# Seven-product blocks in a fixed interleaving, with two of their sums per step made by accumulating transfers

## The chip, the core and the metric

The kernel is one program on one core of a Trainium2 chip. The metric is the device time of one execution, in microseconds, as the median over several executions. The engines are named as in the profile: PE multiplies matrices (PEld is its weight load), DVE and ACT work element by element, POOL here issues the accumulating transfers and a few small operations, and SP issues the plain loads.

## The reference

Two layers of a decoder trunk on 256 tokens of width 2048, all in float32. Cut to what matters here:

```python
for l in range(2):
    h = rms_norm(x, norm1_g[l])
    z = h @ w_in[l]                      # the 1024 query columns of it are one of the blocks below
    ...                                  # gated spatial unit, windowed attention, out projection
    h2 = rms_norm(x, norm2_g[l])
    x = x + (silu(h2 @ w_gate[l]) * (h2 @ w_up[l])) @ w_down[l]     # w_gate, w_up: 2048 x 5632
```

## The kernel before

**The arithmetic.** A weight tile is 128 rows by 1024 values in float32 (two row groups j of 512 columns). `split2` (L117) makes two tiles of it: `wh`, rounded by a cast on ACT (L123), and `wl`, what the rounding left, by a subtraction on DVE (L124). Each product is then three matmuls of 512 columns (`mm3`, L158 to L161): high activations with `wh`, high activations with `wl`, low activations with `wh`. A *half unit* is one weight tile against one token tile: 6 matmuls. A *standard unit* (`unit`, L163) is one weight tile against both token tiles: 12 matmuls.

**Seven products in place of eight.** For the queries of a layer, and for ten of the eleven column blocks of the gate and up projections (`S_BLOCKS`), `seven` (L333) multiplies a 2 x 2 arrangement of activations (token tile by parity of the row group) with a 2 x 2 arrangement of weights (parity r by column block c, `src(r, c, i)`) with seven products in place of eight. There are four steps i, each with one tile of every weight block: b11 = src(0,0), b12 = src(0,1), b22 = src(1,1), b21 = src(1,0). The products need sums of weights: b11+b12, t2 = b11+b12+b22, b12+b22 and t2+b21. The sums of activations (`ext`) were made earlier. The products go into five PSUM banks (m0 to m4), and sums of the banks make the results (`out`, which for the gate and up projections is `gated`, L1057: silu of the one times the other).

**Where the sums are made.** In each step b11+b12 (L365) and t2 (L366) are additions on DVE. b12+b22 is an addition on DVE (L372) or, for the steps named in `by_dma`, a transfer from HBM issued on POOL that adds what it brings to what lies in SBUF (L368). `by_dma` is all four steps for the first layer's queries, steps 0 and 2 for the gate and up blocks, and no step for the second layer's queries. t2+b21 is always such a transfer (L374).

**What sets the order.** Generators yield unit by unit. The stretch of the gate, up and down projections draws half units from `s_stream` (L1069) and fills standard units of `w_down` and of the one remaining block in between, about 3 standard units for 10 half units (L1197). The queries of the first layer run between the standard units of keys, values and gating, at a set pace (`q_to`, L489). `later` puts small work at a set distance. After that a planner of the framework puts the instructions of each engine into a fixed order by its own model of their durations. Each engine and each queue then works through its instructions in that order, and waits at the first one whose inputs are missing.

**Buffers.** 8 tiles `raw` hold weights as loaded, 5 `wh` and 4 `wl` hold the split halves, 4 tiles (`spt`) hold t2. A load on SP waits until the last reader of the tile that was in its buffer is done. PSUM has 5 banks of the kind the seven products use.

Of the kernel before, what the change touches and what calls it, by code (L numbers as in the profile page):

```python
# [12 lines left out]
F32 = mybir.dt.float32  # L13
# [3 lines left out]
ALU = mybir.AluOpType  # L17
# [3 lines left out]
P = 128  # L21
# [13 lines left out]
NB = 512  # L35
# [6 lines left out]
S_BLOCKS = (1, 2, 3, 4, 5, 6, 7, 8, 9, 10)  # L42
# [28 lines left out]
EXT_AT = (6.5, 8, 11, 13, 16, 18, 21.5, 24)  # L71
MASK_AFTER = ((5, 5), (4, 4))
GATE_LOAD = ((24, 29), (5, 15))
PARTS = (
    "a0 a0 a1 a1 s a0 a0 s a1 s a1 s s s b0 s b0 s b0 s b0 s b1 s b1 s b1 s b1 s b2 b2 b2 b2 b3 b3 b3 b3",
    "a0 a0 a1 a1 a0 a0 s a1 a1 s b0 b0 s b0 s b0 s s b1 s b1 s b1 s b1 s s b2 s b2 s b2 b2 s b3 b3 b3 b3",
# [14 lines left out]
def trunk(ctx, tc, x, xt, w_in, w_q, w_out, w_oa, w_uh, w_gate, w_up, w_down, sgu_w, sgu_g, consts,  # L91
          band, out):
    nc = tc.nc
# [14 lines left out]
    def raw_load(src, parts=1):  # L108
        raw = wp.tile([P, 2, NB], F32, tag="raw", name="raw", bufs=8)
        n = 2 // parts  # L110
        for i in range(parts):
            nc.sync.dma_start(raw[:, i * n : (i + 1) * n, :], src[:, i * n : (i + 1) * n, :])
        return raw

    last_wl = [None]

    def split2(raw):  # L117
        wh = wp.tile([P, 2, NB], F32R, tag="wh", name="wh", bufs=5)
        wl = wp.tile([P, 2, NB], F32R, tag="wl", name="wl", bufs=4)
        step = 2 if clock[0] > 1 else 1  # L120
        for j in range(0, 2, step):
            src = raw[:, j : j + step, :]
            nc.scalar.copy(wh[:, j : j + step, :], src)  # L123
            last_wl[0] = nc.vector.tensor_tensor(  # L124
                wl[:, j : j + step, :], src, f(wh[:, j : j + step, :]), ALU.subtract
            )
        return wh, wl
# [5 lines left out]
    def later(delay, fn):  # L133
        pending.append((clock[0] + delay, next(serial), fn))

    def tick(w=1.0):
        clock[0] += w
        due = sorted((e for e in pending if e[0] <= clock[0]), key=lambda e: e[:2])
        pending[:] = [e for e in pending if e[0] > clock[0]]
        for e in due:  # L140
            e[2]()
# [16 lines left out]
    def mm3(acc, ah, al, wh, wl, first, last, again=False):  # L158
        nc.tensor.matmul(acc, ah, wh, start=first, stop=False, skip_group_check=again)  # L159
        nc.tensor.matmul(acc, ah, wl, start=False, stop=False, skip_group_check=again)  # L160
        nc.tensor.matmul(acc, al, wh, start=False, stop=last, skip_group_check=again)  # L161
# [50 lines left out]
    anchor = [None]  # L212
# [120 lines left out]
    def seven(src, pairs, ext, out, end=lambda sg: None, soon=False, by_dma=(), put_off=False):  # L333
# [78 lines left out]
        end([m0, c21])  # L412
        yield

    def seven_low(src, pairs, ext, done, tag="hT"):
        def half(raw, acc, op, i, first=False, stop=False):
            wh, wl = split2(raw)
# [62 lines left out]

    def q_product(lay, pairs, ext):
        q = {"k": 0}
        q["steps"] = seven(
            lambda r, c, i: w_q[lay, c, i, r], pairs, ext, lambda *a: q["out"](*a),
            soon=True, by_dma=range(4 if lay == 0 else 0),
        )
        return q

    def q_to(q, share):  # L489
# [32 lines left out]
    for lay in range(L):  # L522
# [526 lines left out]
        def act_later(b, sg, held=held, release=release):  # L1049
            for c in range(2):  # L1050
                def ready(c=c):
                    held.append((b, c, sg))
                    release()

                later(2 + c, ready)
# [3 lines left out]
            nc.vector.scalar_tensor_tensor(sg, c, nrstd2[t], sg, ALU.mult, ALU.mult)  # L1059

        def s_block(b, lay=lay, pairs2=pairs2, ext2=ext2, gated=gated, act_later=act_later):
            return seven(
                lambda r, c, i: (w_gate, w_up)[c][lay, b, i, r], pairs2, ext2, gated,
                lambda sg: act_later(b, sg), soon=b == S_BLOCKS[0], by_dma=(0, 2), put_off=True,
            )

        seven_done = [False]

        def s_stream(s_block=s_block):  # L1069
            for b in S_BLOCKS:  # L1070
                yield from s_block(b)

        seeds = []
        left = [NFF]
# [230 lines left out]
```

## Time and profile before

| | |
|---|---|
| median of the executions | 1907.07 us (1906.84 to 1908.11, 3 executions) |
| the profiled execution | 1906.77 us, its span 1905.1 us |
| PE busy | 1892.9 us, 99% of the span, 8624 matmuls and transposes |
| DVE busy | 1745.5 us, 92% |
| ACT busy | 1374.7 us, 72% |
| POOL busy | 183.9 us, 10% |
| moved by DMA | 463.12 MB, 243 GB/s |

The span is from the first to the last instruction of the profiled execution. A matmul's busy time is modelled and overlaps the next one's, so the distance of the starts tells more than the busy time. The gate, up and down stretches lie at about 330 to 925 us (first layer) and 1275 to 1870 us (second layer), the first layer's queries at about 30 to 120 us.

### The profile page before, as it was taken

How to read it: one execution, taken by the hardware profiler on the slowest of the kernel's cores; microseconds unless marked ns; L12 is line 12 of the kernel's file. 1: busy time of each engine (PE TensorE's matmuls, PEld its weight loads, DVE VectorE, ACT ScalarE, POOL GpSimd, SP SyncE). 2: the span in 40 equal slices, each digit the busy share in tenths (PEclk: the TensorE clock that was granted, in tenths of full speed). 3: DMA queues.
4: the chain of work that ended last, by engine and by line, in shares of the span. 5: the costliest groups of instructions: out<-in, count | busy, mean ns of one | idle time of the engine just before them, and what ended most of it. 6: DMA issues, size and time to landing. Idle time of an engine off the chain costs nothing.

```text
span 1905.1 us, 25218 instructions
## 1 busy us (share of the span) xinstructions
PE 1892.9 (99%) x8624; PEld 1544.2 (81%) x8624; DVE 1745.5 (92%) x1894; ACT 1374.7 (72%) x1860; POOL 183.9 (10%) x184
## 2 busy tenths in 40 slices
PE   9999999999999999999999999999999999999999
PEld 6887788888888888888888778888888888888887
DVE  7988989999999999999798888999999999999993
ACT  8668777677767776777776886766877677676774
POOL 0231001000100001000002200000000100010000
PEclk9999999999999999999999999999999999999999
DMA  9973668888977897889578648697789788888783
GB/s 356 261 284 133 194 202 243 248 247 276 271 238 245 270 290 228 243 261 290 185 217 291 191 153 237 212 280 224 233 282 288 227 254 264 270 249 251 249 277 110
DMA packets 129153, 463.12 MB, mean 243 GB/s; under 512 B 14336, under 2 KB 14720, under 8 KB 129024
## 3 DMA queue, kind: packets, MB, share of 16 engines
q1 hardware_dynamic: 105840, 378.54, 53.9%
q0 software_dynamic: 22464, 81.80, 23.7%
q8 instruction: 67, 1.10, 0.2%
q10 hardware_dynamic: 720, 1.18, 0.2%
q14 instruction: 62, 0.51, 0.1%
HBM read 459.36 MB, written 2.10 MB: 242 GB/s over the span
## 4 chain that ended last, share of the span: by engine, by line
PE 94%; ACT 2%; DVE 2%; issue 1%; DMA 0%; POOL 0%; SPq 0%; DVEq 0%; ACTq 0%; POOLq 0%
PE m L160 15%; PE m L159 15%; PE m L161 15%; PE dacc L160 11%; PE dacc L159 11%; PE dacc L161 11%; PE acc L160 4%; PE acc L161 3%; PE acc L159 3%; PE l L159 1%; PE l L160 1%; PE l L161 1%; PE ps_f L242 1%; PE ps_n L242 1%; DVE wl L124 1%
## 5 line engine op out<-in xcount | busy, mean ns | idle before, releaser
L123 ACT CAST wh<-raw 128x1024 fp32r<-128x1024 f32 (+1 forms) x794 | 814.0, 1050 | 366.5 <-DVE raw L365 165.7
L124 DVE TENSOR_TENSOR wl<-raw,wh 128x1024 fp32r<-128x1024 f32 (+1 forms) x794 | 943.9, 1217 | 83.0 <-issue 25.5
L159 PE MATMUL m<-wh,ext 128*128 128x512 f32 x704 | 276.7, 393 | 0.0
L160 PE MATMUL m<-wl,ext 128*128 128x512 f32 x704 | 275.0, 391 | 0.0
L161 PE MATMUL m<-wh,ext 128*128 128x512 f32 x704 | 274.4, 390 | 0.0
L160 PE MATMUL dacc<-wl,aT 128*128 128x512 f32 x624 | 243.5, 390 | 0.0
L159 PE MATMUL dacc<-wh,aT 128*128 128x512 f32 x624 | 243.0, 391 | 0.0
L161 PE MATMUL dacc<-wh,aT 128*128 128x512 f32 x624 | 242.9, 389 | 0.0
L124 DVE TENSOR_TENSOR wl<-t,wh 128x1024 fp32r<-128x1024 f32 x176 | 213.1, 1221 | 10.0 <-issue 5.2
L123 ACT CAST wh<-t 128x1024 fp32r<-128x1024 f32 x176 | 184.3, 1051 | 37.0 <-DVE t L366 14.1
L159 PE MATMUL m<-wh,hT 128*128 128x512 f32 x528 | 206.3, 391 | 0.0
L160 PE MATMUL m<-wl,hT 128*128 128x512 f32 x528 | 205.7, 390 | 0.0
L161 PE MATMUL m<-wh,hT 128*128 128x512 f32 x528 | 205.5, 389 | 0.0
L160 PEld LDWEIGHTS m<-wl,ext 128*128 128x128 f32 x704 | 132.2, 188 | 29.1 <-DVE wl L124 2.2
L159 PEld LDWEIGHTS m<-wh,ext 128*128 128x128 f32 x704 | 132.2, 188 | 27.6 <-ACT wh L123 0.8
L161 PEld LDWEIGHTS m<-wh,ext 128*128 128x128 f32 x704 | 132.1, 188 | 27.5
L159 PEld LDWEIGHTS dacc<-wh,aT 128*128 128x128 f32 x624 | 117.1, 188 | 25.0 <-ACT wh L123 0.7
L160 PEld LDWEIGHTS dacc<-wl,aT 128*128 128x128 f32 x624 | 117.2, 188 | 24.7 <-DVE wl L124 0.6
L161 PEld LDWEIGHTS dacc<-wh,aT 128*128 128x128 f32 x624 | 117.1, 188 | 24.2
L374 POOL DMA_DIRECT2D t<-in_w_gate_dram x80 | 69.1, 864 | 525.0 <-DVE wl L124 412.9
L161 PEld LDWEIGHTS m<-wh,hT 128*128 128x128 f32 x528 | 99.1, 188 | 20.6
L159 PEld LDWEIGHTS m<-wh,hT 128*128 128x128 f32 x528 | 99.1, 188 | 20.3
(212 smaller groups left out, 2907.5 us busy)
## 6 DMA issues: line engine op xcount, KB each, us to landing
raw<-in_w_gate_dram SPq DMA_DIRECT2D x176, 512.0 KB, 5.9
raw<-in_w_up_dram SPq DMA_DIRECT2D x176, 512.0 KB, 5.9
raw<-in_w_down_dram SPq DMA_DIRECT2D x176, 512.0 KB, 5.8
t<-in_w_gate_dram POOLq DMA_DIRECT2D x80, 512.0 KB, 7.7
raw<-in_w_in_dram SPq DMA_DIRECT2D x68, 512.0 KB, 6.7
raw<-in_w_out_dram SPq DMA_DIRECT2D x48, 512.0 KB, 4.3
raw<-in_w_up_dram POOLq DMA_DIRECT2D x40, 512.0 KB, 6.5
raw<-in_w_q_dram SPq DMA_DIRECT2D x32, 512.0 KB, 5.7
```

Of the source, the lines that this page charges most:

```text
L123: nc.scalar.copy(wh[:, j : j + step, :], src)
L124: last_wl[0] = nc.vector.tensor_tensor(wl[:, j : j + step, :], src, f(wh[:, j : j + step, :]), ALU.subtract)
L159: nc.tensor.matmul(acc, ah, wh, start=first, stop=False, skip_group_check=again)
L160: nc.tensor.matmul(acc, ah, wl, start=False, stop=False, skip_group_check=again)
L161: nc.tensor.matmul(acc, al, wh, start=False, stop=last, skip_group_check=again)
L242: nc.tensor.transpose(ps[:, j, t * P : (t + 1) * P], blocks[t][:, j * P : (j + 1) * P], ident)
L374: anchor[0] = nc.gpsimd.dma_start(t2, src(1, 0, i), accum_op=ALU.add)
```

## The change

The function `seven` is replaced, for the gate and up blocks of both layers and for the queries of the first layer, by a class `Lean` with one method for each product, and by a table `LEAN` that gives each of the 28 half units of a block (seven products by four steps) its place. Consecutive blocks are laid 28 places apart and overlap: the last product of a block (`four`, places 30 to 37) lies among the first half units of the next. The second layer's queries still use `seven`.

In a step, b12 is no longer loaded into a tile of its own. After `one` has split b11, an accumulating transfer adds b12 to it in place; `five` uses the sum, and after `five` another such transfer adds b12 to b22 in place, for `seven`. t2 is one addition on DVE in `five`. b21 is loaded by SP once, in `two`, is split there, and is added to t2 on DVE. Before, it was brought twice: by a load, and by an accumulating transfer.

So for the gate and up blocks a step has 2 additions on DVE (before 3, or 2 where `by_dma` holds), 2 accumulating transfers (before 1, or 2) and 3 loads on SP (before 4). For the first layer's queries it has 2 additions, 2 accumulating transfers and 3 loads (before 2, 2 and 4). At the end of a block, the addition of m0 to m3 on DVE (L392) gives way to a copy of bank m0 into bank m3 on ACT, on which the third product's matmuls accumulate. The products and the number of matmuls stay as they were.

```diff
@@ -71,6 +71,10 @@
 EXT_AT = (6.5, 8, 11, 13, 16, 18, 21.5, 24)
 MASK_AFTER = ((5, 5), (4, 4))
 GATE_LOAD = ((24, 29), (5, 15))
+LEAN = (
+    (0, 4, 8, 12), (24, 26, 27, 29), (6, 10, 14, 18), (30, 31, 33, 37), (7, 11, 15, 19),
+    (16, 20, 22, 23), (13, 17, 21, 25),
+)
 PARTS = (
     "a0 a0 a1 a1 s a0 a0 s a1 s a1 s s s b0 s b0 s b0 s b0 s b1 s b1 s b1 s b1 s b2 b2 b2 b2 b3 b3 b3 b3",
     "a0 a0 a1 a1 a0 a0 s a1 a1 s b0 b0 s b0 s b0 s s b1 s b1 s b1 s b1 s s b2 s b2 s b2 b2 s b3 b3 b3 b3",
@@ -412,6 +416,107 @@
         end([m0, c21])
         yield
 
+    class Lean:
+        def __init__(self, src, pairs, ext, out, end=lambda sg: None):
+            self.src, self.out, self.end = src, out, end
+            self.bank, self.raw, self.t2, self.z = {}, {}, {}, {}
+
+            def a_op(k, t):
+                return lambda p, h: pairs[p][:, h, k, t * P : (t + 1) * P]
+
+            def e_op(n):
+                return lambda p, h: ext[p][:, h, n, :]
+
+            self.home = {
+                1: (0, a_op(0, 0)), 2: (0, a_op(1, 0)), 3: (4, e_op(3)), 4: (2, a_op(1, 1)),
+                5: (1, e_op(1)), 6: (3, e_op(2)), 7: (2, e_op(0)),
+            }
+
+        def acc(self, m):
+            if m not in self.bank:
+                self.bank[m] = pa.tile([P, NB], F32, tag="acc", name=f"m{m}")
+            return self.bank[m]
+
+        def half(self, n, raw, i):
+            m, op = self.home[n]
+            wh, wl = split2(raw)
+            first, last = n in (1, 3, 5, 7) and i == 0, i == 3
+            for j in range(2):
+                ah, al = (op(2 * i + j, h) for h in range(2))
+                mm3(
+                    self.acc(m), ah, al, wh[:, j, :], wl[:, j, :], first and j == 0,
+                    last and j == 1, m in (0, 2, 3),
+                )
+            tick(0.5)
+
+        def add(self, out, x, y):
+            nc.vector.tensor_tensor(out, x, y, ALU.add)
+
+        def onto(self, dst, i):
+            anchor[0] = nc.gpsimd.dma_start(dst, self.src(0, 1, i), accum_op=ALU.add)
+
+        def one(self, i):
+            self.raw[1, i] = raw_load(self.src(0, 0, i))
+            self.half(1, self.raw[1, i], i)
+            self.onto(self.raw[1, i], i)
+
+        def three(self, i):
+            self.raw[3, i] = raw_load(self.src(1, 1, i))
+            self.half(3, self.raw[3, i], i)
+
+        def five(self, i):
+            self.half(5, self.raw[1, i], i)
+            self.t2[i] = ap.tile([P, 2, NB], F32, tag="spt", name="t2", bufs=4)
+            with tc.issue_after(last_wl[0].ins):
+                self.add(self.t2[i], self.raw[1, i], self.raw[3, i])
+            self.onto(self.raw[3, i], i)
+
+        def six(self, i):
+            if i == 0:
+                nc.scalar.copy(self.acc(3), self.bank[0])
+            self.half(6, self.t2[i], i)
+
+        def seven(self, i):
+            self.half(7, self.raw[3, i], i)
+
+        def two(self, i):
+            b21 = raw_load(self.src(1, 0, i))
+            self.half(2, b21, i)
+            self.add(self.t2[i], self.t2[i], b21)
+            z, bank = self.z, self.bank
+            if i == 0:
+                for v in ("m0", "c12", "c21", "c22"):
+                    z[v] = zp.tile([P, NB], F32, tag="z", name=v)
+                nc.scalar.copy(z["m0"], bank[3])
+            elif i == 1:
+                self.add(z["c21"], bank[2], z["m0"])
+            elif i == 2:
+                nc.scalar.copy(bank[2], z["c21"])
+                self.add(z["c12"], bank[1], z["m0"])
+            else:
+                self.add(z["c22"], bank[1], z["c21"])
+                self.add(z["c12"], bank[4], z["c12"])
+
+        def four(self, i):
+            self.half(4, self.t2[i], i)
+            z, bank = self.z, self.bank
+            if i == 0:
+                self.out(0, bank[0], z["m0"], z["c12"])
+            elif i == 3:
+                later(1, lambda: self.out(1, bank[2], z["c21"], z["c22"]))
+                self.end([z["m0"], z["c21"]])
+
+    def lean_run(blocks):
+        steps = sorted(
+            (28 * n + LEAN[m][i], n, m, i) for n in range(len(blocks)) for m in range(7) for i in range(4)
+        )
+        for _, n, m, i in steps:
+            b = blocks[n]
+            (b.one, b.two, b.three, b.four, b.five, b.six, b.seven)[m](i)
+            yield
+            if m in (3, 5) and i == 3:
+                yield
+
     def seven_low(src, pairs, ext, done, tag="hT"):
         def half(raw, acc, op, i, first=False, stop=False):
             wh, wl = split2(raw)
@@ -480,10 +585,8 @@
 
     def q_product(lay, pairs, ext):
         q = {"k": 0}
-        q["steps"] = seven(
-            lambda r, c, i: w_q[lay, c, i, r], pairs, ext, lambda *a: q["out"](*a),
-            soon=True, by_dma=range(4 if lay == 0 else 0),
-        )
+        args = (lambda r, c, i: w_q[lay, c, i, r], pairs, ext, lambda *a: q["out"](*a))
+        q["steps"] = lean_run([Lean(*args)]) if lay == 0 else seven(*args, soon=True)
         return q
 
     def q_to(q, share):
@@ -1059,16 +1162,15 @@
             nc.vector.scalar_tensor_tensor(sg, c, nrstd2[t], sg, ALU.mult, ALU.mult)
 
         def s_block(b, lay=lay, pairs2=pairs2, ext2=ext2, gated=gated, act_later=act_later):
-            return seven(
+            return Lean(
                 lambda r, c, i: (w_gate, w_up)[c][lay, b, i, r], pairs2, ext2, gated,
-                lambda sg: act_later(b, sg), soon=b == S_BLOCKS[0], by_dma=(0, 2), put_off=True,
+                lambda sg: act_later(b, sg),
             )
 
         seven_done = [False]
 
         def s_stream(s_block=s_block):
-            for b in S_BLOCKS:
-                yield from s_block(b)
+            return lean_run([s_block(b) for b in S_BLOCKS])
 
         seeds = []
         left = [NFF]
```

What stands in each engine's order, at three places. In these rows L124 of the kernel before and L128 of the changed one are the subtraction of `split2`, L365, L366, L372 and L453 additions of whole tiles, L1038 and L1141 the split of the activations for the down projection. Names carry the number of the buffer's tile.

First, DVE in the middle of a gate and up block of the first layer. Before, around the additions of one step:

```order
L124 TENSOR_TENSOR wl_4025<-raw_4017,wh_4024 128x1024
L365 TENSOR_TENSOR raw_4017<-raw_4017,raw_4019 128x1024
L1038 TENSOR_TENSOR aT_3985<-ps_f_3980,aT_3985 128x512
L366 TENSOR_TENSOR t2_4023<-raw_4017,raw_4021 128x1024
L124 TENSOR_TENSOR wl_4037<-raw_4017,wh_4036 128x1024
L124 TENSOR_TENSOR wl_4049<-raw_4046,wh_4048 128x1024
L1038 TENSOR_TENSOR aT_4014<-ps_f_4009,aT_4014 128x512
L372 TENSOR_TENSOR raw_4019<-raw_4019,raw_4021 128x1024
L124 TENSOR_TENSOR wl_4066<-t2_4023,wh_4065 128x1024
L124 TENSOR_TENSOR wl_4077<-raw_3926,wh_4076 128x1024
```

Now, around an addition of `five` and the addition of b21 (`raw_4261`) in `two`:

```order
L128 TENSOR_TENSOR wl_4108<-raw_3963,wh_4107 128x1024
L453 TENSOR_TENSOR t2_4117<-raw_3963,raw_4095 128x1024
L1141 TENSOR_TENSOR aT_4068<-ps_f_4063,aT_4068 128x512
L128 TENSOR_TENSOR wl_4123<-t2_3936,wh_4122 128x1024
L128 TENSOR_TENSOR wl_4133<-raw_3986,wh_4132 128x1024
L128 TENSOR_TENSOR wl_4145<-raw_4142,wh_4144 128x1024
L128 TENSOR_TENSOR wl_4163<-raw_4160,wh_4162 128x1024
L453 TENSOR_TENSOR t2_3936<-t2_3936,raw_4261 128x1024
L128 TENSOR_TENSOR wl_4173<-raw_4039,wh_4172 128x1024
L453 TENSOR_TENSOR t2_4182<-raw_4039,raw_4160 128x1024
```

The three additions of a step, which stood within seven rows, are now one addition per `five`. The addition in `two` is new: it stands six rows behind the addition that last reads `raw_3963`, and `raw_4261` is loaded into the buffer of `raw_3963`.

Second, DVE in the last step of the first layer's queries (L767 and L870 scale the gating values). Before:

```order
L365 TENSOR_TENSOR raw_868<-raw_868,raw_870 128x1024
L768 TENSOR_TENSOR v_670<-v_670,gb_668 128x512
L366 TENSOR_TENSOR t2_874<-raw_868,raw_872 128x1024
L124 TENSOR_TENSOR wl_907<-raw_868,wh_906 128x1024
L124 TENSOR_TENSOR wl_917<-t2_874,wh_916 128x1024
L124 TENSOR_TENSOR wl_930<-raw_927,wh_929 128x1024
L124 TENSOR_TENSOR wl_952<-raw_872,wh_951 128x1024
L124 TENSOR_TENSOR wl_962<-raw_870,wh_961 128x1024
```

Now:

```order
L128 TENSOR_TENSOR wl_856<-raw_650,wh_855 128x1024
L453 TENSOR_TENSOR t2_865<-raw_650,raw_825 128x1024
L453 TENSOR_TENSOR t2_529<-t2_529,raw_975 128x1024
L128 TENSOR_TENSOR wl_869<-t2_629,wh_868 128x1024
L128 TENSOR_TENSOR wl_881<-raw_878,wh_880 128x1024
L870 TENSOR_TENSOR v_668<-v_668,ir16_973 128x512
L453 TENSOR_TENSOR t2_629<-t2_629,raw_1028 128x1024
L128 TENSOR_TENSOR wl_897<-raw_709,wh_896 128x1024
```

The additions of b21 have come in here too: `raw_1028` is loaded into the buffer of `raw_650`, whose last reader is the first addition shown, and its own addition stands five rows later.

Third, the accumulating transfers on POOL at the beginning of the first layer's gate and up blocks (`ir2` is the reciprocal root mean square). Before:

```order
L225 TENSOR_TENSOR ir2_2721<-ms2_2719,mhalf_99 128x2
L368 DMA raw_2862<-in_w_up_dram 128x1024
L374 DMA t2_2866<-in_w_gate_dram 128x1024
L374 DMA t2_2953<-in_w_gate_dram 128x1024
L368 DMA raw_3038<-in_w_up_dram 128x1024
L374 DMA t2_3042<-in_w_gate_dram 128x1024
L374 DMA t2_3117<-in_w_gate_dram 128x1024
```

Now:

```order
L229 TENSOR_TENSOR ir2_2713<-ms2_2711,mhalf_99 128x2
L456 DMA raw_2847<-in_w_up_dram 128x1024
L456 DMA raw_2879<-in_w_up_dram 128x1024
L456 DMA raw_2892<-in_w_up_dram 128x1024
L456 DMA raw_2937<-in_w_up_dram 128x1024
L456 DMA raw_2950<-in_w_up_dram 128x1024
L456 DMA raw_2975<-in_w_up_dram 128x1024
```

Three transfers for two steps have become four, they all bring w_up, and each adds to a tile that one half unit reads before it and another after it.

## The prediction

> **What bounds the kernel now.** I read the page's head and chain first, then busy time by stage, then what PE's weight loads waited for in the gate and up stretches.
>
> ```profile
> span 1905.1 us, 25218 instructions
> PE 1892.9 (99%) x8624; PEld 1544.2 (81%) x8624; DVE 1745.5 (92%) x1894; ACT 1374.7 (72%) x1860; POOL 183.9 (10%) x184
> PEclk9999999999999999999999999999999999999999
> PE 94%; ACT 2%; DVE 2%; issue 1%; DMA 0%; POOL 0%; SPq 0%; DVEq 0%; ACTq 0%; POOLq 0%
> ```
>
> PE has 94% of the chain that ends last, at full clock. A busy PE need not be a PE at its peak, so the starts have to be looked at (timeline of PE; start, length):
>
> ```profile
> 625.71 0.39 PE L159 MATMUL m<-wh,hT 128*128 128x512 f32 x1
> 625.94 0.39 PE L160 MATMUL m<-wl,hT 128*128 128x512 f32 x1
> ...
> 628.43 0.39 PE L159 MATMUL m<-wh,ext 128*128 128x512 f32 x1
> 628.66 0.39 PE L160 MATMUL m<-wl,ext 128*128 128x512 f32 x1
> ```
>
> From 625.71 to 628.43 lie 12 starts, 0.227 us apart. A half unit is then 6 x 0.227 = 1.36 us, a standard unit 2.72 us, and the change touches neither their number nor their size. What is left to win is what PE waits for. In the first layer's stretch, the weight loads' waits (total, times, longest), then the two largest of the second layer's, then the one in the first layer's queries:
>
> ```profile
> PEld ps_f L242 <- DVE aT L1038: 1.5, 4, 0.4
> PEld m L160 <- DVE wl L124: 1.0, 4, 0.4
> PEld dacc L159 <- ACT wh L123: 0.4, 1, 0.4
> PEld m L159 <- ACT wh L123: 0.3, 1, 0.3
> PEld dacc L160 <- DVE wl L124: 0.3, 1, 0.3
> PEld ps_f L242 <- DVE c L1059: 0.3, 1, 0.3
> ```
>
> ```profile
> PEld ps_f L242 <- DVE aT L1038: 1.4, 4, 0.4
> PEld m L160 <- DVE wl L124: 0.8, 3, 0.4
> ```
>
> ```profile
> PEld dacc L160 <- DVE wl L124: 0.4, 1, 0.4
> ```
>
> That is 3.8 us in one layer, much the same in the other, 0.4 in the queries: a ceiling of some 8 us, or 0.4%. Of such a wait the matmuls lose a part only: the start at 390.49 (quoted below) follows a weight load that waited 0.4 us, and the next comes 0.34 instead of 0.227 us later. I take 3 us in all. The kernel is bound by PE, with DVE just behind it:
>
> ```profile
> 360.00:925.00 565.00, 564.98 (x2526) 464.98 (x2525) 537.49 (x504) 405.20 (x476) 44.94 (x52) 1.00 0.84 258
> ```
>
> (Stretch, length, then busy time of PE, PEld, DVE, ACT and POOL, clock, DMA share, GB/s.) DVE is busy for 537.49 of 565.00 us. How far it is ahead of PE shows in its own timeline:
>
> ```profile
> 385.49 0.69 DVE L1038 TENSOR_TENSOR aT<-ps_f,aT 128x512 fp32r<-128x512 f32 x1
> 386.10 1.22 DVE L366 TENSOR_TENSOR t<-raw 128x1024 f32<-128x1024 f32 x1
> 387.23 1.22 DVE L124 TENSOR_TENSOR wl<-raw,wh 128x1024 fp32r<-128x1024 f32 x1
> 388.37 1.22 DVE L372 TENSOR_TENSOR raw<-raw 128x1024 f32<-128x1024 f32 x1
> 389.50 1.22 DVE L124 TENSOR_TENSOR wl<-t,wh 128x1024 fp32r<-128x1024 f32 x1
> ...
> 616.79 4.73 DVE L124 TENSOR_TENSOR wl<-raw,wh 128x1024 fp32r<-128x1024 f32 x4
> ```
>
> ```profile
> 390.49 0.50 PE L159 MATMUL dacc<-wh,aT 128*128 128x512 f32 x1
> 390.83 0.45 PE L160 MATMUL m<-wl,ext 128*128 128x512 f32 x1
> ```
>
> Back to back, a full tile costs DVE 1.13 to 1.14 us (386.10, 387.23, 388.37, 389.50), a half tile 0.61. After the additions the subtraction begun at 389.50 ends at 390.72 and is read at 390.83: a lead of 0.1. After four subtractions without additions the one that ends at 621.52 is read at 625.94 (quoted above): a lead of 4.4. That is about the most: with 4 `wl` buffers a subtraction starts once the unit four before is through, 3 x 1.36 - 1.22 = 2.9 us ahead among half units, 4.2 with one standard unit among the three.
>
> **The change part by part.** *DVE* (rows by line; busy time and mean of one):
>
> ```profile
> L365 DVE TENSOR_TENSOR raw<-raw 128x1024 f32<-128x1024 f32 x88 | 107.7, 1223 | 2.3
> L366 DVE TENSOR_TENSOR t<-raw 128x1024 f32<-128x1024 f32 x88 | 107.6, 1223 | 2.2
> L372 DVE TENSOR_TENSOR raw<-raw 128x1024 f32<-128x1024 f32 x44 | 53.6, 1218 | 0.0
> L392 DVE TENSOR_TENSOR m<-m,m 128x512 f32<-128x512 f32 x22 | 15.1, 685 | 1.3 <-PE m L161 1.2
> ```
>
> Each of the twenty gate and up blocks had 4 + 4 + 2 additions of whole tiles and has 8 now, so 40 go, and with them 21 of L392 (the second layer's queries keep theirs). At the spacing above this is 40 x 1.135 + 21 x 0.61 = 58 us of DVE, none on PE's path. What it buys is the lead: in a block DVE's work falls by 2.9 us. So I let the 3 us of DVE-caused waits go: **-3**. ACT gains 21 copies like this one, 12 us, beside 28% idle time: 0.
>
> ```profile
> L391 ACT COPY m<-m 128x512 f32<-128x512 f32 x22 | 12.7, 576 | 0.0
> ```
>
> *Transfers.* SP issues 84 loads fewer (4 a block), POOL 40 accumulating transfers more (2 a block of gate and up). Their queues' shares:
>
> ```profile
> q1 hardware_dynamic: 105840, 378.54, 53.9%
> q0 software_dynamic: 22464, 81.80, 23.7%
> ```
>
> A MB costs 0.142% of the span on the loads' queue, 0.290% on the accumulating one; with 0.524 MB a transfer, 84 x 0.0746 = 6.3% goes and 40 x 0.152 = 6.1% comes. The DMA engines stay as full as they were: 0.
>
> *What is new is a wait on DVE*, at the addition of b21 in `two`. Landing times, from issue, of SP's loads in the first layer's stretch, of the two accumulating kinds there (L374, L368), and of SP's loads at 84 to 105 us:
>
> ```profile
> DMA to landing us min/median/max: 3.1/6.0/12.5
> DMA to landing us min/median/max: 5.6/7.7/9.3
> DMA to landing us min/median/max: 5.2/6.8/8.6
> DMA to landing us min/median/max: 3.3/9.4/11.1
> ```
>
> In the first place shown in the order, `raw_4261` can be issued when the addition that reads `raw_3963` ends, and the addition that needs it comes one half tile and four whole ones later: 0.61 + 4 x 1.135 = 5.2 us. At the median DVE waits 6.0 - 5.2 = 0.8 us. Counted through the order, 32 of the 80 such additions in the gate and up blocks have 3.4 to 5.7 us of DVE work in front, the rest 6.8 or more. So DVE loses 1 to 2 us in each of these, two or three in a cluster. Around `raw_4261`, from the subtraction of `raw_3963` to the last addition of the cluster, stand 11 subtractions, 5 additions and a half tile: 16 x 1.135 + 0.61 = 18.8 us of DVE against 9 half and 2 standard units, 17.7 us of PE. That takes 1.1 of a lead of 2.9 to 4.2 and leaves 1.8 to 3.1 for waits of 0.8 each: PE is touched only where a load takes 7 us or more. From below this costs 0 (every load at 3.1 lands in time); from above, if each of the 32 lands at 7.7 like an accumulating one, a wait of about 2.9 each less a remaining lead of 2.4 leaves 0.5 x 32 = 16. I take **+2**, near the lower end, since the median is 6.0.
>
> Behind the waiting addition stand the subtractions of the next units, and PE waits for those. In the second place, in the first layer's queries, the addition of `raw_1028` has 3 whole tiles and a half one in front: 3 x 1.135 + 0.61 = 4.0. A landing of 3.3 costs nothing; at 9.4 DVE waits 5.4, and after a lead of 2.9 PE stands 2.5. I take **+1.5**, between.
>
> *The accumulating transfers' distance.* The cast behind them on ACT:
>
> ```profile
> L123 ACT CAST wh<-raw 128x1024 fp32r<-128x1024 f32 x790 | 811.6, 1052 | 366.3 <-DVE raw L365 165.7 <-PE dacc L161 87.4 <-PE acc L161 36.1
> ```
>
> b11 is split in `one` and used again in `five`, seven places later: in full flow mostly 13.6 us of matmuls lie between, at the least 8.2, with the 1.36 of `one` itself 9.5; the transfer needs 7.7, the cast and the subtraction behind it 1.05 and 1.22, 10 together, and a lead of 2.9 to 4.2 comes on top of the 9.5. In the first block of each layer the places between are empty: 5.5 us of matmuls lie between `one` and `five`, 6.8 with those of `one` itself. With a lead of 2.9 to 4.2 that is 9.7 to 11.0 against 10: 0 to 1 us, twice; **+0.5**. The cast's largest wait, 165.7 us for L365, goes with L365 and costs PE nothing now.
>
> The sum: 1906.77 - 3 + 2 + 1.5 + 0.5 = 1907.8, a microsecond above this execution's own time, which is 0.3 below the median of the runs. I predict **1907.8 us**.
>
> **The rivals.** *Faster.* DVE is relieved, the loads land in time, and all waits quoted go: 1906.8 - 8 = 1899 at most, 1902.5 with 4.3 us and nothing new. For it: DVE is the releaser in most of those rows. Against it: the rows hold too little, and the b21 additions are new. 9%.
>
> *Slower: b21 is late on DVE.* This decides once loads issued beside an accumulating transfer land at about 6.8 us rather than 6.0; the spread up to 12.5 speaks for it, and that `raw_4261` is issued at the very addition that also releases an accumulating transfer. Against it: there are fewer loads. Between 0 and 16 us, half way 8, plus 2.5 in the queries: 1906.8 - 3 + 8 + 2.5 = 1914. 22%.
>
> [...] 5%, counted as no change.
>
> [...]
>
> *The change does nothing that can be measured*, which is my forecast: PE is full and stays so. 64%, with the 5% above 69%.
>
> **How the numbers follow.** About 0.2%, 3.8 us, is what a measurement here can tell from no change. Faster 9%, same 69%, slower 22%. The likeliest case's own range is 1904 to 1911; to leave out no more than 2 in 10, I reach into both rivals: 1903 to 1913.
>
> **What would show it.** DVE busy near 1690 us; no L365-like wait on ACT, and instead a wait of DVE's additions (L453) for SP's loads of w_gate, tens of microseconds in total. PE's starts still 0.227 apart, weight-load waits on DVE's `aT` and `wl` under 4 us a layer. At 80 to 100 us a PE wait of 1 to 3 us behind a load of w_q. Wrong it would be if PE's waits in the gate and up stretches exceed 5 us a layer (late b21, or casts that wait for accumulating transfers), or if the span falls below 1901, which would mean that PE's pace itself hung on DVE.

## The result, and the profile after

The changed kernel takes 1934.56 us, the median of 4 runs (1929.91 to 1939.34); the kernel before took 1907.59 beside it. The ratio is 1.0142, with a 95% interval of 1.0113 to 1.0171: slower by 1.4%, some 27 us. The forecast was 1907.8 us, no change. The time lies outside the range of 1903 to 1913 and beyond the 1914 given to the rival that b21 comes late.

The page of the changed kernel begins thus (the profiled execution took 1937.19 us):

```profile
span 1935.5 us, 25400 instructions
...
PE 1901.4 (98%) x8624; PEld 1544.7 (80%) x8624; DVE 1685.3 (87%) x1833; ACT 1401.2 (72%) x1881; POOL 212.5 (11%) x224
...
PE 83%; DVE 5%; DMA 4%; ACT 4%; issue 3%; POOL 1%; SPq 0%; DVEq 0%; ACTq 0%; POOLq 0%
```

DVE has the 60 us less that were forecast (1685.3 after 1745.5), PE has the same 8624 instructions, and still PE's share of the chain that ends last fell from 94% to 83%: DVE, ACT and transfers stand on it now. PE executes the same number of instructions in both kernels, and only in two kinds of place in another order, so its starts can be compared by instruction number. This table is worked out from PE's records in the two traces:

| PE instructions | what they are | before, us | after, us | change |
|---|---|---|---|---|
| 0 to 439 | start and the first layer's queries | 104.2 | 111.6 | +7.4 |
| 439 to 1311 | rest of attention | 178.2 | 178.2 | 0.0 |
| 1311 to 3983 | 284 to 882 us of before: most of it the first layer's gate, up and down | 598.3 | 611.3 | +13.1 |
| 3983 to 5555 | 882 to 1214 us: end of that stretch, the second layer's attention | 331.3 | 332.5 | +1.2 |
| 5555 to 8227 | 1214 to 1811 us: the second layer's gate, up and down | 597.1 | 606.9 | +9.8 |
| 8227 to the end | the tail | 94.4 | 93.3 | -1.1 |

The sum is the 30.4 us by which the two spans differ. The profiled execution is 2.6 us above the median of its kernel, and the executions of the changed kernel lie up to 9.4 us apart, so the parts are those of these two executions. What the engines waited for, over the whole changed kernel (total, times, longest):

```profile
POOL raw L456 <- DVE t L453: 304.8, 42, 17.2
...
DVE t L453 <- DMA raw<-in_w_gate_dram: 55.7, 21, 5.2
...
ACT wh L127 <- DMA raw<-in_w_up_dram: 35.0, 26, 2.6
...
PEld m L164 <- DVE wl L128: 19.8, 22, 2.8
...
PEld ps_f L246 <- DVE aT L1141: 8.2, 6, 2.3
...
PEld dacc L164 <- DVE wl L128: 6.1, 8, 1.2
```

Two rows are new in kind. `DVE t L453 <- DMA raw<-in_w_gate_dram` is the addition of b21 in `two`, waiting for its load. `ACT wh L127 <- DMA raw<-in_w_up_dram` is the cast of a buffer that an accumulating transfer has not finished. The last three rows are what PE's weight loads waited for behind them.

**One place with a late b21.** Timeline of DVE in the changed kernel (start, length, in brackets the idle time before it and what ended it), and then of PE:

```profile
891.01 1.23 DVE L128 TENSOR_TENSOR wl<-raw,wh 128x1024 fp32r<-128x1024 f32 x1 [0.19 <-PE m L164]
896.89 1.23 DVE L453 TENSOR_TENSOR t<-t,raw 128x1024 f32<-128x1024 f32 x1 [4.65 <-DMA raw<-in_w_gate_dram]
898.03 2.35 DVE L128 TENSOR_TENSOR wl<-raw,wh 128x1024 fp32r<-128x1024 f32 x2
900.30 1.22 DVE L453 TENSOR_TENSOR t<-raw 128x1024 f32<-128x1024 f32 x1
901.44 1.22 DVE L128 TENSOR_TENSOR wl<-t,wh 128x1024 fp32r<-128x1024 f32 x1
```

```profile
897.78 0.39 PE L163 MATMUL m<-wh,ext 128*128 128x512 f32 x1
899.30 0.50 PE L164 MATMUL m<-wl,ext 128*128 128x512 f32 x1 [1.13 <-DVE wl L128]
```

The load was issued at 888.01 and landed 8.8 us later. DVE stood 4.65 us at the addition. The subtraction that follows it had had its cast since 892.2, and PE needed it at 898.0; it came at 899.2. With this one wait and the additions behind it, PE lost 1.4 us here and 1.4 more in the next 6 us. Twenty-one such waits make up the row of 55.7; eight of them are 4.3 to 5.2 us long, behind loads that landed in 8.2 to 9.9 us.

**One place with a late accumulating transfer.** From the chain of waits of the changed kernel (start, length):

```profile
579.21 1.23 DVE t L453
...
580.96 7.98 DMA raw<-in_w_up_dram
...
589.04 1.06 ACT wh L127
590.09 0.49 ACT xres L1236
...
591.13 0.58 ACT xres L1236
...
592.55 0.59 ACT m L490
593.14 0.50 ACT dacc L1210
593.64 0.04 issue
593.68 0.50 PE dacc L163
```

In `five` the sum b11 + b12 + b22 is taken at 579.21. The transfer that adds b12 to b22 may start only behind it (its row on POOL: `POOL raw L456 <- DVE t L453`), lands after 7.98 us, and only then can ACT cast the tile for `seven`. Behind that cast on ACT stand the copies that hand the down projection's accumulator to PE, which waited for the last of them at 593.68.

Landing times, from issue, in the first layer's stretch, for SP's loads and for the accumulating transfers:

```profile
DMA to landing us min/median/max: 3.2/5.6/10.1
...
DMA to landing us min/median/max: 5.3/8.1/11.2
```

The loads' median is better than the 6.0 of before. The median was not what mattered.

### The profile page after: what moved, and what is told of

Same layout as the page of the kernel before. It is cut to its first block, busy times and chain, and to the rows that moved or that the text cites. A ratio compares the mean times of both kernels' runs of the same rounds, so it can differ in the third digit from the quotient of the medians.

```text
span 1935.5 us, 25400 instructions
## 1 busy us (share of the span) xinstructions
PE 1901.4 (98%) x8624; PEld 1544.7 (80%) x8624; DVE 1685.3 (87%) x1833; ACT 1401.2 (72%) x1881; POOL 212.5 (11%) x224
## 4 chain that ended last, share of the span: by engine, by line
PE 83%; DVE 5%; DMA 4%; ACT 4%; issue 3%; POOL 1%; SPq 0%; DVEq 0%; ACTq 0%; POOLq 0%
PE m L164 13%; PE m L165 12%; PE m L163 12%; PE dacc L164 10%; PE dacc L163 10%; PE dacc L165 10%; PE acc L164 3%; PE acc L165 3%; PE acc L163 3%; DVE wl L128 3%; DMA raw<-in_w_up_dram 2%; ACT wh L127 1%; PE l L163 1%; PE l L164 1%; PE l L165 1%
## 5 line engine op out<-in xcount | busy, mean ns | idle before, releaser
L127 ACT CAST wh<-raw 128x1024 fp32r<-128x1024 f32 (+1 forms) x794 | 823.0, 1051 | 341.2 <-PE dacc L165 173.0
L128 DVE TENSOR_TENSOR wl<-raw,wh 128x1024 fp32r<-128x1024 f32 (+1 forms) x794 | 949.0, 1217 | 117.1 <-ACT wh L127 46.9
L456 POOL DMA_DIRECT2D raw<-in_w_up_dram x160 | 138.5, 867 | 1078.0 <-DVE wl L128 371.9
L128 DVE TENSOR_TENSOR wl<-t,wh 128x1024 fp32r<-128x1024 f32 x176 | 212.2, 1218 | 8.2 <-ACT wh L127 4.8
L127 ACT CAST wh<-t 128x1024 fp32r<-128x1024 f32 x176 | 184.5, 1052 | 47.5 <-PE m L165 30.6
L453 DVE TENSOR_TENSOR t<-t,raw 128x1024 f32<-128x1024 f32 x84 | 103.0, 1230 | 58.5 <-DMA raw<-in_w_gate_dram 55.7
L164 PEld LDWEIGHTS m<-wl,hT 128*128 128x128 f32 x528 | 99.2, 188 | 21.6 <-DVE wl L128 1.6
```

Source lines behind the costliest of these rows:

```text
L128: last_wl[0] = nc.vector.tensor_tensor(wl[:, j : j + step, :], src, f(wh[:, j : j + step, :]), ALU.subtract)
L453: nc.vector.tensor_tensor(out, x, y, ALU.add)
L456: anchor[0] = nc.gpsimd.dma_start(dst, self.src(0, 1, i), accum_op=ALU.add)
```

## The experiments

Three explanations were open. First, **DVE's order**: the addition of b21 stands ahead of subtractions that are ready, and its load is late. Second, **the distance of the accumulating transfers**: they land too late for the casts by themselves. Third, what makes the loads of b21 late: the accumulating transfers beside them, or a late issue.

### The addition of b21 behind its own subtraction

```diff
             self.half(2, b21, i)
-            self.add(self.t2[i], self.t2[i], b21)
+            with tc.issue_after(last_wl[0].ins):
+                self.add(self.t2[i], self.t2[i], b21)
```

> The changed kernel, with one thing moved: the addition of b21 in `two` is held until the subtraction of b21 itself has been issued on DVE. It still adds the same tiles, but no longer stands ahead of the subtractions of other units. First theory, DVE's order: PE stands because subtractions that are ready queue behind an addition that waits for its load (55.7 us of such waits, the long ones 4.3 to 5.2 each); then these waits fall below 10 us, PE's lost time in the two gate and up stretches falls from some 23 us to under 8, and the time to 1910 to 1917. Rival, the accumulating transfers: they land at 8.2 us in the median and up to 11, too late for the casts of `five` and `seven` by themselves; then the additions stop waiting but PE's stalls stay in their greater part, and the time is 1922 to 1932.

Measured: 1917.36 us, ratio 1.0050 (1.0035 to 1.0065). 17.2 of the 27 us are gone. No wait of an addition for in_w_gate is left among that run's waits. In the same stretch of work, DVE went on while the same load was under way (issued at 874.09, landed 8.2 us later):

```profile
877.07 3.95 DVE L128 TENSOR_TENSOR wl<-raw,wh 128x1024 fp32r<-128x1024 f32 x3 [0.19 <-PE m L164]
880.94 1.22 DVE L453 TENSOR_TENSOR t<-raw 128x1024 f32<-128x1024 f32 x1
882.51 1.23 DVE L128 TENSOR_TENSOR wl<-t,wh 128x1024 fp32r<-128x1024 f32 x1 [0.36 <-issue]
```

By stages against the kernel before: +0.2 in the queries (after +7.4), +4.2 in the first layer's stretch (after +13.1), +5.7 in the second's (after +9.8). So DVE's order is the larger cause, and with it goes all but 0.2 us of the queries' loss. What is left shows in these rows of that run:

```profile
ACT wh L127 <- DMA raw<-in_w_up_dram: 40.9, 30, 3.8
...
PEld ps_f L246 <- DVE aT L1142: 10.2, 10, 2.0
...
PEld m L164 <- DVE wl L128: 5.3, 8, 2.2
```

By the transfer that each cast waited for, 33.5 of these 40.9 us are casts of `seven` and the rest casts of `five`. The expectation of 1910 to 1917 was met at its upper edge; the rival's statement, that the late casts cost time by themselves, is right for the rest.

### Without the additions of b21

```diff
-            self.add(self.t2[i], self.t2[i], b21)
```

> The changed kernel without the 84 additions of b21 (the load of b21 and its own product stay, the sum that `four` uses lacks b21). DVE has 84 x 1.135 = 95 us less and no wait on these loads; the accumulating transfers are all there. DVE's order as the cause: 1900 to 1907, since DVE then has 5 us a block to spare. The accumulating transfers as the cause: at least half of the 27 us stay, 1920 or more, with ACT's waits for in_w_up at 30 us as they are.

Measured: 1910.19 us (1.0006 to 1.0025). It lies between the two forecasts: most of the loss goes with these additions, but with DVE at 1605.8 us of work and the waits of `PEld m` for `wl` down to 0.4 us, 2.6 us remain. ACT's waits for in_w_up are 20.3 us in that run, not the 30 expected.

### The new scheme in the gate and up blocks alone

```diff
-        q["steps"] = lean_run([Lean(*args)]) if lay == 0 else seven(*args, soon=True)
+        q["steps"] = seven(*args, soon=True, by_dma=range(4 if lay == 0 else 0))
```

> The new scheme in the gate and up blocks alone; the first layer's queries as they were before the change. The queries' part of the loss in the trace is 7.4 us (the first 439 instructions of PE take 111.6 us and took 104.2). If the parts add up, the time is 1934.6 - 7.4 = 1927, within the spread of the changed kernel (1923 to 1932); if the queries' delay is given back later or makes the blocks' delays, it differs from that by more than 4 us.

Measured: 1928.86 us (1924.57 to 1930.66), 5.7 below the changed kernel. The queries' part is 0.2 under that of before, the two stretches lose 9.7 and 9.0. The parts add up within the spread of the runs.

### Without the accumulating transfers

```diff
-            anchor[0] = nc.gpsimd.dma_start(dst, self.src(0, 1, i), accum_op=ALU.add)
+            pass
```

> The changed kernel without its 164 accumulating transfers (`five` and `seven` split b11 and b22 as they are, so b12 is left out of the sums). The additions of b21 stay where they stand on DVE. If the lateness of b21 is made by the accumulating transfers in flight (loads land at 3.2 to 3.6 us alone, 8 to 9 beside two of them), the loads now land at 3.5 to 5 us, the additions' waits go from 55.7 us to under 10, and the time is 1902 to 1908. If b21 is late because its load is issued late, whatever else is in flight, 20 us of waits or more stay, and the time is above 1915.

Measured: 1905.09 us, ratio 0.9985 (0.9976 to 0.9994). The additions stand on DVE where the changed kernel has them, yet they hardly wait:

```profile
DVE t L453 <- DMA raw<-in_w_gate_dram: 4.8, 7, 1.1
...
DVE t L453 <- DMA raw<-in_w_q_dram: 1.5, 1, 1.5
```

So the loads are late because of the accumulating transfers in flight, not because they are issued late. The traces say the same of the two parts of a wait: the loads of w_gate that made an addition wait had been issued 3.8 to 6.8 us before the wait began in the changed kernel, and 3.9 to 4.9 us before it in this run; what fell is their landing, from 8.2 to 9.9 us in the eight longest waits there to 4.3 to 5.7 us in all seven here. From issue and landing of each transfer in the changed kernel's gate and up stretches (330 to 930 and 1290 to 1910 us): with one other load of SP in flight, a load lands after 3.6 us (median of 56) with no accumulating transfer in flight at its issue, 5.7 (81) with one, 8.5 (23) with two. In the kernel before it was 3.4, 5.9 and 8.1. Without its transfers the changed kernel is 2.5 us faster than the one before, but then it leaves out b12.

### More places from `five` to `seven`

A second table of places, used in the gate and up blocks; rows are the products one to seven, and in each the places of its four steps:

```diff
-    (0, 4, 8, 12), (24, 26, 27, 29), (6, 10, 14, 18), (30, 31, 33, 37), (7, 11, 15, 19),
-    (16, 20, 22, 23), (13, 17, 21, 25),
+    (0, 4, 6, 9), (24, 26, 27, 29), (7, 11, 13, 15), (30, 31, 33, 38), (8, 12, 14, 16),
+    (18, 19, 20, 22), (17, 21, 23, 25),
```

> As the run that holds the addition of b21 behind its own subtraction (1917.4 us), and in the gate and up blocks a second table of places: from `five` to `seven` 9 places instead of 6, from `one` to `five` 7 or 8 instead of 7; the queries keep the changed kernel's table. What is left over the kernel before, some 10 us, is put down to the accumulating transfer of `five`, which is needed by the cast of `seven` (8.0 us to landing, 7.3 to 8.1 us from its issue to that cast where it is tight; ACT waits 36 us for such transfers in that run). Three places more are 3 x 1.36 = 4.1 us: ACT's waits for in_w_up fall below 8 us, and the time to 1906 to 1910. Rival, not distance but the load on the DMA engines: the transfers stretch with what is in flight, the waits stay above 20 us and the time at 1913 or more.

> The changed kernel with the second table of places in the gate and up blocks (from `five` to `seven` 9 places), the additions of b21 where the changed kernel has them on DVE. If the two causes add up, this takes away the 10 us of the transfers of `five` and leaves the 17 of the additions: 1923 to 1927. If most of the lateness of b21 comes from the late casts, it takes more: below 1920.

Measured: 1919.21 us with the addition held (1.0040 to 1.0073), 1932.54 without (1.0109 to 1.0139). The first theory's forecasts failed in both runs, and so did the other forecast for the second, below 1920. With the addition held, the rival's figures came true (waits above 20 us, 1913 us or more), but most of these waits are not the ones that it spoke of. The casts of `seven` wait no more (0 us), so the distance does what it should. But the table puts the four steps of `one` within nine places, and their transfers now run beside those of `five`: in the run with the addition held six casts of `five` wait 17.1 us, where they waited 7.5, behind transfers that take 9 to 11 us. The other 25.6 us of the first row are twelve casts that wait for plain loads of w_up, and ACT also waits for loads of the down projection (second row); with the changed kernel's table and the addition held these were 0 and 2.1 us:

```profile
ACT wh L131 <- DMA raw<-in_w_up_dram: 42.8, 18, 5.4
...
ACT wh L131 <- DMA raw<-in_w_down_dram: 9.0, 8, 2.6
```

One wait was exchanged for others, among them waits for plain loads.

### One kind of transfer left out

```diff
-            self.onto(self.raw[3, i], i)
```

> As the run that holds the addition of b21 behind its own subtraction, without the accumulating transfers of `five` (so `seven` multiplies b22 alone, b12 is left out of that sum); those of `one` stay. If the transfers of `five` are what is left, 1905 to 1909. If any accumulating transfer in flight does it, about half of the 10 us stays: 1912.

```diff
-            self.onto(self.raw[1, i], i)
```

> The same without the accumulating transfers of `one` instead (so `five` and the sums after it lack b12); those of `five` stay. If distance from `five` to `seven` is what counts, ACT's waits for in_w_up stay at 20 us or more and the time at 1912 to 1917; if the number of accumulating transfers in flight counts, half of them stretch the others less, the waits fall by more than half and the time is 1909 or less.

Measured: 1904.20 us without the transfers of `five` (0.9965 to 0.9986), 1913.52 without those of `one` (1.0013 to 1.0034); 1917.36 with both. In the first run ACT waits for in_w_up once, 0.4 us, though the 80 transfers of `one` in the blocks are all there; in the second it is this:

```profile
ACT wh L127 <- DMA raw<-in_w_up_dram: 28.8, 20, 3.6
```

So most of what is left over the kernel before is the way from `five` to `seven`: without the transfers of `one` its transfers are still too late. They take 7.8 us to landing in the median then, and 8.2 with the others there, so those of `one` stretch them little; what goes with those of `one` is 3.8 us of time, and the 7.5 us for which casts of `five` waited.

How much a late cast costs depends on DVE too. With all transfers there but no additions of b21, the two stretches take 2.0 and 1.6 us more than before, against 1.5 and 1.0 less without the transfers: 6.1 us for them. With the additions held it is 12.3 (+4.2 and +5.7 against -1.4 and -1.0 without the transfers of `five`).

### `seven` later, with the transfers spread as before

```diff
-    (0, 4, 8, 12), (24, 26, 27, 29), (6, 10, 14, 18), (30, 31, 33, 37), (7, 11, 15, 19),
-    (16, 20, 22, 23), (13, 17, 21, 25),
+    (0, 4, 8, 12), (24, 26, 27, 29), (6, 10, 13, 17), (30, 31, 33, 37), (7, 11, 15, 19),
+    (16, 18, 21, 23), (14, 20, 22, 25),
```

> As the run that holds the addition of b21 behind its own subtraction (1917.4 us), with a third table of places in the gate and up blocks: `one` and `five` stay where the changed kernel has them, so the accumulating transfers are issued as evenly as there; only `seven` moves back, to 7, 9, 7 and 6 places after `five` instead of 6 each. If the time from `five` to `seven` is what is short and the earlier table failed because it drew the transfers of `one` and `five` together, the 30 us for which the casts of `seven` wait fall to 10 to 20, those of `five` stay at 6 or less, and the time is 1911 to 1915. If moving `seven` helps nothing, because some other work stands behind it, 1916 or more.

Measured: 1913.79 us, ratio 1.0037 (1.0023 to 1.0051). The casts of `seven` wait 13.0 us instead of 33.5, a fall as expected; those of `five` 16.4 instead of 7.5, more than expected. The longest wait is 2.2 us instead of 3.8. The time came out in the range given, but its interval overlaps that of the run it is compared with, so the 3.6 us between them are not certain; the stages agree (+2.0 and +4.5 instead of +4.2 and +5.7).

### b12 by load and addition instead of the transfer of `five`

```diff
             self.raw[3, i] = raw_load(self.src(1, 1, i))
+            if i in (1, 3):
+                self.b12[i] = raw_load(self.src(0, 1, i))
...
-            self.onto(self.raw[3, i], i)
+            if i in self.b12:
+                later(1, lambda: self.b12_add(i))
+            else:
+                self.onto(self.raw[3, i], i)
```

> As the run that holds the addition of b21 behind its own subtraction (1917.4 us); in addition b12 reaches b22 for two of four i (1 and 3) by a plain load, issued in `three`, and an addition on DVE two half units after `five`, behind a subtraction, instead of the accumulating transfer of `five`. DVE gets 42 x 1.135 = 48 us more (1733 in all, under the 1745 of the kernel before), POOL 42 transfers fewer. If the late transfers of `five` are the rest of the loss, half of it goes or more, since the others overlap less: 1908 to 1911. If DVE's fill counts as much as the transfers, no gain: 1915 or more.

> The same for all four i: only the transfers of `one` are left to POOL, and DVE has 84 x 1.135 = 95 us more than in the changed kernel, 1780 in all, 35 more than the kernel before. If only late transfers cost PE time: 1904 to 1907, as without the transfers of `five` (1904.2). If a full DVE does too: its lead shrinks in the clusters of additions and PE waits for subtractions again, 1910 or more, above the run with two of four.

Measured: 1926.31 us with two of four i (1.0078 to 1.0108), 1949.74 with all (1.0197 to 1.0227). The first theory failed in both runs, and the rival, a fuller DVE, had named only lower bounds (1915 and 1910 us) far under what was measured. The landing time of the transfers does fall (to 6.4 us in the median in the second run), and SP's loads land faster too (4.6 us in the first layer's stretch, 5.6 in the changed kernel). But in the second run this row is the largest of its kind:

```profile
ACT wh L127 <- DMA raw<-in_w_down_dram: 47.1, 24, 4.9
```

Loads that land faster and still come too late are issued too late: these had been issued 1.5 to 6.5 us before the wait began. All loads take turns in the same 8 `raw` buffers, and each b12 holds one more from `three` until its addition. In the first layer's stretch of the second run SP's loads wait 37 times for these additions, 41.1 us in all, a row that the run with the addition of b21 held has not. That this is what delays the issue was not tried by itself, and DVE's added work (1768.8 us busy against 1686.0) came in with it; it is the likeliest reading, not shown. The granted clock fell too: it was 0.993 of full speed over the second run, and 1.000 with the addition held. Half clock for eight times 3.4 us in all (last section) is worth at most some 13 of the 41 us lost, an estimate at 1.6 us each.

### The sum of `five` ahead of its subtraction

```diff
-            self.half(5, self.raw[1, i], i)
             self.t2[i] = ap.tile([P, 2, NB], F32, tag="spt", name="t2", bufs=4)
-            with tc.issue_after(last_wl[0].ins):
-                self.add(self.t2[i], self.raw[1, i], self.raw[3, i])
+            self.add(self.t2[i], self.raw[1, i], self.raw[3, i])
+            self.half(5, self.raw[1, i], i)
```

> As the run that holds the addition of b21 behind its own subtraction, with the sum of `five` (b11 + b12 + b22) written ahead of the subtraction of `five` instead of behind it. The transfer of `five` waits for that sum, so it is issued one subtraction, 1.14 us, earlier; the subtraction comes 1.14 us later. If the time from `five` to `seven` is what is short, ACT's waits for in_w_up (36 us in that run) fall by a third or more and the time by 2 to 5 us, to 1912 to 1916. If DVE's own order is as tight, the later subtraction of `five` costs as much: 1917 or more.

Measured: 2022.52 us, ratio 1.0601 (1.0533 to 1.0669). The first theory's forecast was off by 106 us; the other's, 1917 or more, holds in its letter and says nothing of this size. The scheduler, free to place it, puts the sum early in DVE's order, where it waits for the transfer of `one`:

```profile
DVE t L453 <- DMA raw<-in_w_up_dram: 124.0, 37, 6.3
```

This is the first cause again, on another addition and larger: 37 waits in DVE's order, 124.0 us in all. The granted clock fell to 0.979 here; 25 times 3.4 us at half clock are worth at most 40 of the 113 us lost, by the same estimate.

No version that computes the whole beat the kernel before. The best of them takes 1913.8 us.

## Why the prediction was wrong

**What held.** PE bounds the kernel (busy for 98% of the span) and its pace is unchanged: 0.227 us from start to start in the median of both traces. DVE fell to 1685 us (about 1690 forecast). The additions of b21 wait for loads of w_gate, 55.7 us in all (tens of microseconds forecast). The term of -3 was about right in size: without the late work (the run without the transfers of `five`) the two gate and up stretches and the tail are 3.6 us shorter than before.

**The step that failed: +2 for the addition of b21.** It was priced at a landing of 6.0 us, the median of all loads, hence a wait of 0.8 us each. Holding the addition back takes 8.9 + 4.1 = 13 us from the two stretches: the term was 13, not 2. The error is the duration that was put in. A load of b21 is issued at the addition in `five` whose end also lets an accumulating transfer go, so it is just these loads that fly beside such transfers (5.7 us with one, 8.5 with two in the counts above; 8.2 to 9.9 in the eight long cases, with one to three in flight at their issue) and do not land at the median over all. The eight long waits were 4.3 to 5.2 us each, where a lead of 2.9 to 4.2 was counted on. The upper bound given, 16, with each of these loads at 7.7 us, came near the truth by luck: it took 32 waits alike, and there were 21, eight of them long. The prediction named the coincidence, in its rival, and gave it too little weight.

**+1.5 for the queries.** Measured 7.1 (the stage's 7.4 less the 0.2 that stay when the addition is held). 4.3 of it is lost at one place of the kind that was forecast, for 80 to 100 us, with a cost that was not in the sum. In the chain of the changed kernel:

```profile
90.71 7.28 DMA raw<-in_w_q_dram
...
98.09 0.10 DVE t L453
...
100.59 1.22 DVE wl L128
101.81 0.04 issue
101.86 0.68 PE m L164
```

No matmul starts between 99.06 and 101.86, and the next eight run at half pace (last section): another 1.6 us. Another 1.8 us go at 63 us, where PE waits for ACT and a cast there had waited 1.6 us for a plain load of w_q that took 12.0 us to land, and 1.3 between 80 and 90 us. These go too when the addition is held; by which way is not shown.

**+0.5 for the distance of the accumulating transfers.** The prediction worked out the way from `one` to `five`, seven places, and left out the way from `five` to `seven`. That one is six places, and its transfer cannot start at the cast: it waits for the sum on DVE, which stands behind a subtraction. With the prediction's own rows and the 8 us to landing measured here, 1.22 + 1.14 on DVE, 8, 1.05 for the cast and 1.22 for the subtraction are 12.6 us, against 6 x 1.36 = 8.2 and a lead of 2.9 to 4.2. Measured: 5.6 + 6.7 = 12.3 us over both stretches (with the addition held, against the run without these transfers); part of that hangs on how full DVE is, as the run without the additions of b21 shows.

With the measured terms the sum is -3.6 + 13 + 7.1 + 12.3 = 28.8; the two profiled spans differ by 30.4, the medians by 27.0.

**The rivals.** The slower one had the right mechanism, and its price of 1914 was half way between its bounds; it lacked the second cause. No delay on POOL showed: the issue of an accumulating transfer there took 863 ns in the median before (L374, at 360 to 925 us, where DVE was busy for 537.5 of the 565 us) and takes 863 ns now (L456). The signs at the prediction's end were good ones: "PE's waits in the gate and up stretches exceed 5 us a layer (late b21, or casts that wait for accumulating transfers)" is what happened. It names both causes; the sum priced the first too low and left the link from `five` to `seven` out of the second.

## What to carry to other kernels

An operation that is not urgent must not stand in an engine's order in front of one that is: DVE stood 4.65 us at such an addition while a subtraction behind it was ready; one line that holds an addition behind the subtraction that needs the same load was worth 17 us, and one addition set free cost 100. Price a wait by the landing time in the place where that transfer is issued (what else is in flight then), not by the median over all, and when a chain of transfers is checked for distance, check each link, from what really releases it. Where the sum of two such waits cannot be excluded, the forecast belongs nearer to the upper bound.

## What the hardware showed that was not expected

**PE ran at half clock after a short standstill.** After the 2.8 us standstill at 99.06 in the changed kernel (stretch, length, busy PE, PEld, DVE, ACT, POOL, granted clock, DMA share, GB/s):

```profile
101.80:104.00 2.20, 2.14 (x5) 1.71 (x6) 2.20 (x3) 0.00 (x0) 0.00 (x0) 0.55 0.95 352
104.00:106.00 2.00, 2.00 (x7) 1.58 (x6) 2.00 (x3) 1.53 (x2) 0.00 (x0) 0.64 1.00 373
106.00:110.00 4.00, 4.00 (x20) 3.27 (x19) 3.39 (x4) 3.04 (x4) 0.00 (x0) 1.00 0.88 258
```

The next eight starts are about 0.427 us apart instead of 0.227; the trace records half clock from 102.01 to 105.42. These eight late starts cost 1.6 us on top. Over the 14 traces of this study, none of 60 standstills of 1.3 to 2.15 us (start to start) was followed by half clock, and 32 of 44 longer ones were. In the changed kernel's own trace three were longer: the one of 2.80 us at 99.06, and two that half clock did not follow, of 2.35 us at 171.38 and of 2.30 us at 820.23.

Every stretch at half clock in these traces, but for the last at the end of each execution, lasts 3.413 us or a whole multiple of it. The clock's switches in the changed kernel are recorded at 6.44, 102.01, 105.42 and 1934.97 us, which lie 28, 1 and 536 times 3.413 us apart; the two in the kernel before, at 4.55 and 1905.77 us, lie 557 times that apart.

Length alone does not decide. One standstill of 2.35 us in the first layer's attention, the same in all 14 traces (171.38 us in the changed kernel, 164.02 in the kernel before), was followed by half clock in five. What decides is not shown.

**Plain loads land later beside accumulating transfers**, in the changed kernel by 2.1 us with one in flight and 2.8 more with two (3.6, 5.7 and 8.5 us above). Without these transfers the median in the first layer's stretch is 3.5 us; it was 5.6.

**The two kinds of accumulating transfer behave differently.** With the addition held, those of `one` land after 5.4 us in the median where no other accumulating transfer is in flight (29), and after 10.2 with others before and behind them (40). Those of `five` take 8.0 us (11) and 8.4 (40), and still 7.9 where the transfers of `one` are left out (58 without another in flight). Why these are slow even so stays open.
